# Expert weights: a place's down matrix is loaded behind the next place's gate and up matrices

## The chip, the cores and the metric

The kernel runs on one core of one Trainium2 chip. The metric is device time in microseconds (us) of one launch, as the median over several runs. Profile times count from the start of the profiled span. Engines are named as the profile names them: PE (TensorE, matrix products), DVE (VectorE), ACT (ScalarE), POOL (GpSimd), SP (SyncE, which here issues nearly all weight loads); "SPq" in a row is SP's own instruction stream.

## What is computed

One step of a one-layer decoder for 512 prompt tokens and 32 sample tokens: a combined input projection, an mLSTM branch, a windowed attention branch, a merge, a layer norm, a mixture of experts, a second norm, a gated embedding, a third norm. The change lies in the mixture of experts alone:

```
def expert_block(args):
    xblk, e = args
    h = jax.nn.silu(xblk @ w_gate[e]) * (xblk @ w_up[e])
    return h @ w_down[e]
...
y = jnp.zeros((M + 1, D), jnp.float32).at[row_tok].add(yb.reshape(P, D).astype(jnp.float32) * row_w[:, None])
```

There are 32 experts. Each token goes to two of them, so 544 tokens make 1088 rows. Of one expert the gate and the up matrix are 1024 x 512 in float32 and the down matrix is 512 x 1024: three times 2 MB.

## The kernel before

**Places, slots, items.** The experts that have tokens are put in an order that the chip works out from the routing; position p in it is a "place". Here there are 27 places, 0 to 26. Each place has one or more "items" of up to 32 rows; 50 items in all. A place's weights lie in one of `NB = 4` slots of SBUF, and place p uses slot p mod 4 as far as place 23; the last three places, 24 to 26, use slots 1, 2 and 3. In the profile, slots 0 and 1 are both called `w`; slot 2 is `w2a` (gate and up, first half of the contraction), `w2b` (second half) and `w2d` (down); slot 3 is `gu3a`, `gu3b` and `r_p`. The loads of places 0 to 3 are issued ahead of the loop; this document speaks of places 4 to 26.

**What TensorE does.** `items_of` walks through the items of a place. For one item, `gate_up` multiplies the first half (32 products, line L299), then the second half (32 more). Then comes the down product (`down`, 16 products, L310) of the item *before* this one: if the item is not the first of its place, that is an item of the same place and needs the same place's down matrix; if it is the first, it is the last item of the place before. So TensorE frees a slot in the order: first gate/up half (semaphore `gh`), second half (`gu`), and, one item later, the down matrix (`dn`). TensorE waits for weights by slot: `gu`*s* and `gv`*s* for the two gate/up halves, `wd`*s* and `we`*s* for the two halves of the down matrix.

**What SP does.** One load is 1 MB; gate and up of one half are two loads (`load_gu`, L135), the down matrix two loads (`load_dn`, L141). `load_place(s, p, before)` reads the number of the expert and the count of items up to the last place of this slot (`value`, L185), waits until TensorE has done so many first halves, issues 2 MB, waits for so many second halves, issues 2 MB, waits for the down product, issues 2 MB. It is called for places 4, 5, 6, ... in turn: a loop `Fori` over full turns of four slots, then straight code for the last, possibly partial turn (`gap` says how many slots it leaves out; here 1). SP works in order, so each wait also holds up every load behind it. Once the last place is loaded, SP issues the `late` loads (L229), and after the experts' last stores the tail begins.

Of the kernel before, what the change touches and what calls it, by code (L numbers as in the profile page):

```python
# [42 lines left out]
NB = 4  # L43
# [88 lines left out]
def load_gu(eng, W, s, w, e, half):  # L132

    ks = slice(KD // 2 * half, KD // 2 * (half + 1))
    return [eng.dma_start(out=W[s][half][:, i], in_=w[i][bass.ds(e, 1)].rearrange("a (p k) f -> (a p) k f", p=P)[:, ks])  # L135
            for i in range(2)]


def load_dn(eng, W, s, w, e, half):
    ks = slice(2 * half, 2 * half + 2)  # L140
    return eng.dma_start(out=W[s][2][:, ks], in_=w[2][bass.ds(e, 1)].rearrange("a (p k) d -> (a p) k d", p=P)[:, ks])  # L141
# [10 lines left out]
def expert_phase(tc, pool, psum, ident, meta, slots, x1, W, w, ybuf, spare, gcol, late, rows, spreads, xs, any_):  # L152
# [12 lines left out]
    sp, pe, act, dve, gp = nc.sync, nc.tensor, nc.scalar, nc.vector, nc.gpsimd  # L165
# [14 lines left out]
    with tc.tile_critical(no_gpsimd_drain=True):  # L180
        S = {n: nc.alloc_semaphore("x_" + n) for n in names}

        def value(e, i, lo, hi, n=1):
            src = meta[0:1, i:i + n] if isinstance(i, int) else meta[0:1, bass.ds(i, n)]
            _, out = nc.values_load_multi_w_load_instructions(  # L185
                src, engines=[e.engine], min_val=lo, max_val=hi,
                skip_runtime_bounds_check_because="the chip made it within bounds")
            return out if n > 1 else out[0]
# [6 lines left out]
            d.then_inc(S[f"gv{NB - 1}"], 16)  # L195
        npos, turns, gap = value(sp, 80, NB, 32), value(sp, 81, 0, 32 // NB - 1), value(sp, 84, 0, NB - 1)

        def load_place(s, p, before):
            e = value(sp, p, 0, 31)
            cnt = value(sp, before, 1, 66)  # L200
            for half, n in enumerate(("gu", "gv")):
                sp.wait_ge(S["gh" if half == 0 else "gu"], cnt)
                for d in load_gu(sp, W, s, w, e, half):
                    d.then_inc(S[f"{n}{s}"], 16)
            sp.wait_ge(S["dn"], sp.snap(cnt + 1))
            for half, n in enumerate(("wd", "we")):
                load_dn(sp, W, s, w, e, half).then_inc(S[f"{n}{s}"], 16)

        with sp.If(turns > 1):
            with sp.Fori(1, turns) as a:  # L210
                for s in range(NB):
                    p = sp.snap(a * NB + s)
                    load_place(s, p, sp.snap(p + (41 - NB)))
        with sp.If(turns > 0):
            for s in range(NB):
                def load_last():
                    p = sp.snap(npos - (NB - s))
                    load_place(s, p, sp.snap(p + gap + (41 - NB)))

                if s < NB - 1:  # L220
                    with sp.If(gap < s + 1):
                        load_last()
                else:
                    load_last()

        for s, loads in late:
            sp.wait_ge(S["dn"], sp.snap(value(sp, sp.snap(npos + (41 - NB + s)), 1, 66) + 1))
# [133 lines left out]
        npp, full, gap = value(pe, 80, NB, 32), value(pe, 81, 0, 32 // NB - 1), value(pe, 84, 0, NB - 1)  # L361
# [8 lines left out]
        for s in range(NB):  # L370
            p = pe.snap(npp - (NB - s))
# [145 lines left out]
def tile_decoder_step(ctx: ExitStack, tc: tile.TileContext, *aps):  # L517
# [1546 lines left out]
    with ExitStack() as scope:  # L2064

        SP_ = pool("spare", stack=scope)
        spare = SP_.tile([P, D], F32, name="xg"), SP_.tile([P, 2, KD, P], F32, name="xg4")
        gather = gp.indirect_dma_start(out=spare[0], out_offset=None, in_=x1d[:], in_offset=bass.IndirectOffsetOnAxis(ap=tok0[:, 0:1], axis=0))
        with tc.issue_after(gather.ins):
            gp.tensor_copy(out=edge[:, 0:1], in_=r_p[:, 0, 0:1])  # L2070
        for _ in prefetch(3, (2,)):
            pass
        expert_phase(tc, pool("xwork", side="right", stack=scope), pool("expp", space=PSUM, stack=scope), ident, meta,
                     (tok, yrow, ywt, shift1, gain1), x1d[:], w_tiles, w_e, ybuf[:], spare, gcol8, late, gb, spreads, x1s,
                     keep[:, 0:256])
# [225 lines left out]
```

## Time and profile before

| | us |
|---|---|
| median of 3 runs | 1129.75 |
| lowest and highest | 1129.23, 1131.23 |
| the profiled execution's own time | 1130.72 |
| its span in the profile | 1128.8 |

The time of the profiled execution is 1.9 us more than its span and 1.0 us more than the median. The expert phase takes the span from about 654 to 1040 us. Ahead of it lie the projections and branches, bound by PE; behind it lies a tail of about 80 us.

Rows of a timeline read: start, duration, engine, line, operation, what is written and read, count, and in brackets the idle time of that engine just before with what ended it. Rows of windows give busy time and count of PE, PEld, DVE, ACT and POOL, then the granted PE clock, the DMA engines' share and GB/s.

### The profile page before, as it was taken

To read this page: it belongs to the slowest core of one execution; us is meant where nothing else is said; L and a number is where in the kernel's file an instruction comes from. 1 tells how busy PE (TensorE), PEld (TensorE's weight loads), DVE (VectorE), ACT (ScalarE), POOL (GpSimd) and SP (SyncE) were. 2 spreads that over 40 slices of the span, in tenths; PEclk is the share of its full clock that TensorE was granted. 3 is DMA by queue.
4 is the path that set the end of the run, shared out by engine and by line. 5 is a ranking of instruction groups with operands and counts; after the bars stand their busy time and mean duration, and the time that the engine had idled before them with its cause. 6 is when DMAs were issued, how large, how long until landed. Compare 5 with 4: busy or idle time off the path is not lost.

```text
span 1128.8 us, 26851 instructions
## 1 busy us (share of the span) xinstructions
PE 1024.6 (91%) x10341; PEld 825.0 (73%) x10342; DVE 494.2 (44%) x1255; ACT 346.8 (31%) x703; POOL 253.3 (22%) x387
## 2 busy tenths in 40 slices
PE   8999999999999999999999867685999778868887
PEld 8988999999877779999989435352666545545765
DVE  5545543546545555565565612110222112113787
ACT  5411223223576565423213211110222112103431
POOL 5000000401346462313401202210222202122021
PEclk9999999999999999999999989896999989889899
DMA  7222222223314323753396979999999999998711
GB/s 251 76 76 64 87 75 75 80 75 112 101 38 150 112 95 132 241 158 77 101 391 258 416 301 417 425 419 427 419 424 421 422 424 421 425 416 361 287 47 62
DMA packets 92305, 264.19 MB, mean 234 GB/s; under 512 B 11486, under 2 KB 58740, under 8 KB 71460
## 3 DMA queue, kind: packets, MB, share of 16 engines
q1 hardware_dynamic: 77332, 231.82, 53.3%
q0 software_dynamic: 10384, 27.67, 6.8%
q10 hardware_dynamic: 4512, 3.64, 1.1%
q8 instruction: 53, 0.87, 0.3%
q14 instruction: 24, 0.20, 0.0%
HBM read 248.96 MB, written 20.13 MB: 238 GB/s over the span
## 4 chain that ended last, share of the span: by engine, by line
PE 70%; DMA 14%; SPq 8%; DVE 4%; issue 4%; ACT 1%; DVEq 0%; POOL 0%; ACTq 0%; POOLq 0%
PE pj L674 14%; PE pj L676 13%; PE pj L675 13%; PE psG L299 9%; SPq L135 5%; DMA w2b<-in_w_eu_dram 5%; DMA gu3b<-in_w_eu_dram 5%; PE psY L310 4%; PE tp L1269 2%; SPq L141 2%; PE sp L1315 1%; PE nm L1303 1%; PE sp L732 1%; DMA w<-ybuf 1%; DMA wg_in<-in_w_in_dram 1%
## 5 line engine op out<-in xcount | busy, mean ns | idle before, releaser
L674 PE MATMUL pj<-xH,wH 128*128 128x256 f32 (+1 forms) x672 | 197.6, 294 | 0.1
L676 PE MATMUL pj<-xH,wL 128*128 128x256 f32 (+1 forms) x672 | 197.4, 294 | 0.0
L675 PE MATMUL pj<-xL,wH 128*128 128x256 f32 (+1 forms) x672 | 195.6, 291 | 0.0
L561 ACT CAST wH<-raw 128x1024 fp32r<-128x1024 f32 x76 | 79.7, 1048 | 232.3 <-PE pj L675 148.2
L674 PEld LDWEIGHTS pj<-xH,wH 128*128 128x128 f32 x672 | 126.5, 188 | 5.5 <-issue 3.8
L676 PEld LDWEIGHTS pj<-xH,wL 128*128 128x128 f32 x672 | 126.4, 188 | 5.5 <-issue 5.1
L675 PEld LDWEIGHTS pj<-xL,wH 128*128 128x128 f32 x672 | 127.1, 189 | 2.0 <-issue 1.5
L562 DVE TENSOR_TENSOR wL<-raw,wH 128x1024 fp32r<-128x1024 f32 x76 | 95.2, 1252 | 69.4 <-ACT wH L561 69.2
L448 DVE COPY xT<-xg 128x256 f32 x49 | 15.3, 313 | 246.1 <-PE psG L299 246.1
L422 ACT ACTIVATE sg<-psG 128x128 f32<-128x128 f32 x50 | 13.9, 277 | 270.9 <-PE psG L299 270.9
L299 PE MATMUL psG<-w,xT 128*32 128x256 f32 x1152 | 72.2, 406 | 25.0 <-issue 18.1
L299 PEld LDWEIGHTS psG<-w,xT 128*32 128x32 f32 x1152 | 43.2, 116 | 52.7 <-issue 34.5
L1291 POOL TENSOR_SCALAR lg<-lg,sm 128x256 f32<-128x256 f32 (+1 forms) x64 | 55.8, 884 | 32.6 <-DVE sm L1288 28.7
L264 POOL DMA_INDIRECT ybuf<-ysb,idy x50 | 49.9, 998 | 45.3 <-POOL idy L261 41.2
L299 PE MATMUL psG<-gu3a,xT 128*32 128x256 f32 x576 | 37.4, 402 | 14.7 <-DMA gu3a<-in_w_eu_dram 9.3
L299 PE MATMUL psG<-w2a,xT 128*32 128x256 f32 x448 | 32.1, 434 | 17.8 <-DMA w2a<-in_w_eu_dram 13.8
L674 PE MATMUL pj<-wH,xH 128*128 128x256 f32 x160 | 47.3, 296 | 0.0
L404 ACT ACTIVATE xg<-psX,gcol 128x128 f32 (+1 forms) x100 | 36.3, 469 | 31.4 <-PE psX L292 31.4
L676 PE MATMUL pj<-wH,xL 128*128 128x256 f32 x160 | 44.8, 280 | 0.0
L675 PE MATMUL pj<-wL,xH 128*128 128x256 f32 x160 | 44.8, 280 | 0.0
L299 PE MATMUL psG<-gu3b,xT 128*32 128x256 f32 x576 | 37.8, 405 | 6.8 <-DMA gu3b<-in_w_eu_dram 6.8
L299 PEld LDWEIGHTS psG<-gu3a,xT 128*32 128x32 f32 x576 | 20.7, 113 | 29.0 <-issue 22.2
(619 smaller groups left out, 2245.0 us busy)
## 6 DMA issues: line engine op xcount, KB each, us to landing
w<-in_w_eg_dram SPq DMA_DIRECT2D x26, 1024.0 KB, 24.0
w<-in_w_eu_dram SPq DMA_DIRECT2D x26, 1024.0 KB, 27.6
w<-in_w_ed_dram SPq DMA_DIRECT2D x26, 1024.0 KB, 28.5
raw<-in_w_in_dram SPq DMA_DIRECT2D x22, 1024.0 KB
w2d<-in_w_ed_dram SPq DMA_DIRECT2D x14, 1024.0 KB, 29.2
r_p<-in_w_ed_dram SPq DMA_DIRECT2D x14, 1024.0 KB, 27.3
w2a<-in_w_eg_dram SPq DMA_DIRECT2D x7, 1024.0 KB, 28.7
w2a<-in_w_eu_dram SPq DMA_DIRECT2D x7, 1024.0 KB, 28.4
```

The costliest lines, as they stand in the source:

```text
L135: return [eng.dma_start(out=W[s][half][:, i], in_=w[i][bass.ds(e, 1)].rearrange("a (p k) f -> (a p) k f", p=P)[:, ks]) for i in range(2)]
L141: return eng.dma_start(out=W[s][2][:, ks], in_=w[2][bass.ds(e, 1)].rearrange("a (p k) d -> (a p) k d", p=P)[:, ks])
L264: gp.indirect_dma_start(out=ybuf.rearrange("t (q d) -> (t q) d", q=4), out_offset=bass.IndirectOffsetOnAxis(ap=idy[:, r:r + 1], axis=0), i ...
L299: m = pe.matmul(psG[32 * q:32 * q + 32], xT[:, k], W[s][half][:, :, kh, P * q:P * q + P], start=k == 0, stop=k == KD - 1)
L310: m = pe.matmul(psY[32 * q:32 * q + 32], hT[:, 32 * k:32 * k + 32], W[s][2][:, k, 256 * q:256 * q + 256], start=k == 0, stop=k == 3)
L404: m = act.activation(out=out, in_=psX[:, k], func=AF.Identity, bias=gcol[:, 1, k:k + 1], scale=gcol[:, 0, k:k + 1])
L561: act.copy(out=H, in_=src)
L562: return eng.tensor_tensor(out=L, in0=src, in1=H.bitcast(F32), op=ALU.subtract)
L674: pe.matmul(out, lh(k), rh(k), start=start and i == 0, stop=False)
L675: pe.matmul(out, lh(k), rl(k), start=False, stop=False)
L676: pe.matmul(out, ll(k), rh(k), start=False, stop=stop and i == len(ks) - 1)
L1291: gp.tensor_scalar(out=lg[:, par, j, 0:nk], in0=lg[:, par, j, 0:nk], scalar1=sm[:, 2, par, j:j + 1], scalar2=None, op0=ALU.mult)
```

## The change

`load_place` is split into `load_up` (gate and up, both halves) and `load_down`. SP now issues, for each place p, first its gate and up matrices, and then the down matrix of place p-1, which lies in the slot before. The very first place of the loop has no down load behind it, and the last place's down load is issued by itself at the end. Waits, semaphores and loads are the same in number and kind; TensorE's, VectorE's, ScalarE's and GpSimd's programs are unchanged. SP reads two more values for each place.

```diff
-        def load_place(s, p, before):
+        def load_up(s, p, before):
             e = value(sp, p, 0, 31)
             cnt = value(sp, before, 1, 66)
             for half, n in enumerate(("gu", "gv")):
                 sp.wait_ge(S["gh" if half == 0 else "gu"], cnt)
                 for d in load_gu(sp, W, s, w, e, half):
                     d.then_inc(S[f"{n}{s}"], 16)
-            sp.wait_ge(S["dn"], sp.snap(cnt + 1))
+
+        def load_down(s, p, before):
+            e = value(sp, p, 0, 31)
+            sp.wait_ge(S["dn"], sp.snap(value(sp, before, 1, 66) + 1))
             for half, n in enumerate(("wd", "we")):
                 load_dn(sp, W, s, w, e, half).then_inc(S[f"{n}{s}"], 16)
...
                 for s in range(NB):
                     p = sp.snap(a * NB + s)
-                    load_place(s, p, sp.snap(p + (41 - NB)))
+                    load_full(load_up, s, p)
+                    if s:
+                        load_full(load_down, s - 1, sp.snap(p - 1))
+                    else:
+                        with sp.If(a > 1):
+                            load_full(load_down, NB - 1, sp.snap(p - 1))
...
+                with sp.If(gap < s + 1) if s < NB - 1 else nullcontext():
+                    load_last(load_up, s)
+                    if s:
+                        with sp.If(gap < s):
+                            load_last(load_down, s - 1)
+                    with sp.If((gap - s) * (gap - s) < 1):
+                        first_of_turn()
+            load_last(load_down, NB - 1)
```

On SP, in the loop, from the down load of slot 2 on (`w2d`) to the gate and up loads of slot 3 (`gu3a`, `gu3b`); place 22 is one that uses this slot 2, and place 23 follows it in slot 3. Before:

```order
L141 DMA w2d<-in_w_ed_dram 128x2048 [waits x_dn]
L141 DMA w2d<-in_w_ed_dram 128x2048
L185 ISA
L185 TENSOR_LOAD meta
L185 ISA
L185 TENSOR_LOAD meta
L135 ISA [waits x_gh]
L135 DMA gu3a<-in_w_eg_dram 128x2048
L135 DMA gu3a<-in_w_eu_dram 128x2048
L135 ISA [waits x_gu]
L135 DMA gu3b<-in_w_eg_dram 128x2048
L135 DMA gu3b<-in_w_eu_dram 128x2048
```

The same place in SP's program with the change:

```order
L135 ISA [waits x_gh]
L135 DMA gu3a<-in_w_eg_dram 128x2048
L135 DMA gu3a<-in_w_eu_dram 128x2048
L135 ISA [waits x_gu]
L135 DMA gu3b<-in_w_eg_dram 128x2048
L135 DMA gu3b<-in_w_eu_dram 128x2048
L185 TENSOR_LOAD meta x2
L208 REGISTER_ALU
L141 ISA [waits x_dn]
L141 DMA w2d<-in_w_ed_dram 128x2048
L141 ISA
L141 DMA w2d<-in_w_ed_dram 128x2048
```

The two down loads have moved behind four gate and up loads, and behind the two waits ahead of those (`x_gh`, `x_gu`).

On SP, the start of the loop: the end of slot 0's gate and up loads (`w_6264`), and what stands between them and the loads of slot 1 (`w_6265`). Before:

```order
L135 DMA w_6264<-in_w_eu_dram 128x2048
L205 REGISTER_ALU
L141 DMA w_6264<-in_w_ed_dram 128x2048 [waits x_dn]
L141 DMA w_6264<-in_w_ed_dram 128x2048
L185 ISA
L185 TENSOR_LOAD meta
L185 ISA
L185 TENSOR_LOAD meta
L135 ISA [waits x_gh]
L135 DMA w_6265<-in_w_eg_dram 128x2048
```

With the change, the block from the first branch to the second is jumped over in the loop's first turn:

```order
L135 DMA w_6264<-in_w_eu_dram 128x2048
L227 COMPARE_AND_BRANCH
L185 ISA
L185 TENSOR_LOAD meta
L185 ISA
L185 TENSOR_LOAD meta
L208 REGISTER_ALU
L141 ISA [waits x_dn]
L141 DMA r_p<-in_w_ed_dram 128x2048
L141 ISA
L141 DMA r_p<-in_w_ed_dram 128x2048
L227 UNCONDITIONAL_BRANCH
```

What follows at once there is the reading of values and the wait `x_gh` of slot 1: in the first turn SP no longer waits for a down product between the loads of place 4 and of place 5.

More of the change, by code (lines that the diff above doesn't have):

```diff
@@ L204, in load_place, with load_full, load_last @@
                     d.then_inc(S[f"{n}{s}"], 16)
-            sp.wait_ge(S["dn"], sp.snap(cnt + 1))
+        def load_down(s, p, before):
+            e = value(sp, p, 0, 31)
+            sp.wait_ge(S["dn"], sp.snap(value(sp, before, 1, 66) + 1))
             for half, n in enumerate(("wd", "we")):
                 load_dn(sp, W, s, w, e, half).then_inc(S[f"{n}{s}"], 16)
+        def load_full(load, s, p):
+            load(s, p, sp.snap(p + (41 - NB)))
+        def load_last(load, s):
+            p = sp.snap(npos - (NB - s))
+            load(s, p, sp.snap(p + gap + (41 - NB)))
         with sp.If(turns > 1):
@@ L212, in expert_phase, with first_of_turn @@
                     p = sp.snap(a * NB + s)
-                    load_place(s, p, sp.snap(p + (41 - NB)))
+                    load_full(load_up, s, p)
[4 more added lines that the diff above has]
+                            load_full(load_down, NB - 1, sp.snap(p - 1))
         with sp.If(turns > 0):
             for s in range(NB):
[L216 to L224, printed above, removed]
+                def first_of_turn():
+                    with sp.If(turns > 1):
+                        load_full(load_down, NB - 1, sp.snap((turns * NB + 31) & 31))
+                with sp.If(gap < s + 1) if s < NB - 1 else nullcontext():
[6 more added lines that the diff above has]
+            load_last(load_down, NB - 1)
         for s, loads in late:
```

## The prediction

> **What bounds the kernel now.** I began with the slices of the page, to see which resource is full where.
>
> ```profile
> PE   8999999999999999999999867685999778868887
> DMA  7222222223314323753396979999999999998711
> GB/s 251 76 76 64 87 75 75 80 75 112 101 38 150 112 95 132 241 158 77 101 391 258 416 301 417 425 419 427 419 424 421 422 424 421 425 416 361 287 47 62
> ```
>
> A slice is 28.2 us. From slice 24 on (about 677 us) the DMA engines move 416 to 427 GB/s until about 1020 us: full, whatever the order of the loads. So bytes set the rate, and the change adds none. What an order can change are three things: idle time at the start, the moment at which a given matrix lands, and idle time that comes when SP is held up. Next I read the start in windows of 2 us, with SP's and PE's rows.
>
> ```profile
> 670.00:672.00 2.00, 2.00 (x36) 1.18 (x32) 0.07 (x1) 0.28 (x1) 0.00 (x0) 0.87 0.87 365
> 672.00:674.00 2.00, 1.30 (x27) 0.54 (x16) 0.92 (x4) 0.00 (x0) 0.00 (x0) 1.00 0.17 66
> 674.00:676.00 2.00, 1.79 (x36) 1.35 (x40) 0.38 (x1) 0.00 (x0) 0.00 (x0) 1.00 0.86 201
> 676.00:678.00 2.00, 2.00 (x44) 1.48 (x40) 0.00 (x0) 0.07 (x1) 0.00 (x0) 1.00 0.98 406
> ```
>
> ```profile
> 661.76 0.43 SPq L135 DMA_DIRECT2D w<-in_w_eu_dram  x1
> 673.36 1.08 SPq L141 DMA_DIRECT2D w<-in_w_ed_dram  x2
> 675.44 0.33 SPq L135 DMA_DIRECT2D w<-in_w_eg_dram  x1
> ```
>
> ```profile
> 665.41 6.16 PE L299 MATMUL psG<-w,xT 128*32 128x256 f32 x64 [4.27 <-issue]
> 671.39 1.91 PE L310 MATMUL psY<-w,hT 128*32 128x256 f32 x32
> ```
>
> The engines run dry: against 422 GB/s the four windows lose (57 + 356 + 221 + 16) x 2 us = 1300 KB, or 3.1 us; I use 3.0. SP had issued place 4's gate and up by 662.2, then stood in the wait for place 0's down product, which ended at 673.30 (671.39 + 1.91). Place 1's gate/up product had freed its first half long before: 6.16 us from 665.41, the first half done at about 669. From issue at 673.36 to full flow after 676 pass about 2 us.
>
> Then the places. Items can be read off PE's rows: a second item of one place uses the same tiles. Place 11 has eight (`gu3a` from 782 to 830), place 22 has five (`w2a` from 961 to 994). Around place 22:
>
> ```profile
> 955.81 1.94 PE L310 MATMUL psY<-w,hT 128*32 128x256 f32 x32
> 960.80 3.52 PE L299 MATMUL psG<-w2a,xT 128*32 128x256 f32 x32 [3.05 <-DMA w2a<-in_w_eu_dram]
> 966.90 3.12 PE L299 MATMUL psG<-w2b,xT 128*32 128x256 f32 x32 [2.58 <-DMA w2b<-in_w_eu_dram]
> 969.77 2.47 PE L310 MATMUL psY<-w,hT 128*32 128x256 f32 x32
> 974.07 1.94 PE L299 MATMUL psG<-w2b,xT 128*32 128x256 f32 x32
> 975.80 1.94 PE L310 MATMUL psY<-w2d,hT 128*32 128x256 f32 x32
> ```
>
> These are the last waits of PE for a weight load. From 969.77 on PE works or waits for its own program, up to the last down product, the last store of rows and the tail:
>
> ```profile
> 1037.81 1.93 PE L310 MATMUL psY<-r_p,hT 128*32 128x256 f32 x32 [1.42 <-DVE ysb L460]
> 1041.61 1.47 POOL L264 DMA_INDIRECT ybuf<-ysb,idy  x1 [0.86 <-POOL idy L261]
> 1048.04 0.81 SPq L2099 DMA_DIRECT2D w<-ybuf  x2
> ```
>
> So the time follows from when place 22's first own down product is done (975.80 + 1.94 = 977.74): all behind it is a chain of PE, then the store, then the tail.
>
> **The change, term by term.** *Counts.* No load, wait or PE instruction is added; SP reads two more values for each place. In a full stretch its issues last 2 us and more since they wait for room, so this is hidden; if the queue were empty it would cost some 0.6 us (SP's rows around 675: 674.44 to 675.44 for two reads and their register work).
>
> *The gap at 672 (-3.0 us on every later landing).* SP now goes from place 4's loads straight to place 5's first half, free at about 669. That is 2 us before the queue runs dry, which is what a load needs to flow, so I take the whole gap as filled. Bounds: 0 if the gap only moves, -3.1.
>
> *Where each matrix lands.* Up to the end of the loop gate and up come 2 MB earlier and the down matrix 4 MB later. What 4 MB are worth here is read from place 22's down matrix and place 23's gate and up, which now go ahead of it. The issues, then the landing times of slot 2's down loads and of the second-half loads of slot 3:
>
> ```profile
> 940.03 4.47 SPq L141 DMA_DIRECT2D w2d<-in_w_ed_dram  x2
> 953.62 2.40 SPq L135 DMA_DIRECT2D gu3b<-in_w_eu_dram  x1
> ```
>
> ```profile
> L141 SPq DMA_DIRECT2D w2d<-in_w_ed_dram x2: 1986/2188/2390, 940.0 to 942.1; - x2
> DMA to landing us min/median/max: 29.3/29.4/29.6
> ```
>
> ```profile
> L135 SPq DMA_DIRECT2D gu3b<-in_w_eu_dram x1: 2398/2398/2398, 953.6 to 953.6; - x1
> DMA to landing us min/median/max: 28.0/28.1/28.2
> ```
>
> The down matrix landed at 942.1 + 29.6 = 971.7, place 23's last up load at 953.6 + 28.2 = 981.8. Taking the landing order as the order of issue, the down matrix now lands where that load did: 10.1 us later. The Trainium skill (DMA: Bandwidth & Descriptors, Queues, rings and completion order) says that each DMA engine consumes its ring in order, while completion is not ordered over the engines; by that the sum stays as it is, and the waits above, ended in the order of issue, agree.
>
> A place with one item loses nothing by that, since its down product comes after the next place's gate/up product anyway. A place with several items needs its own down matrix right after its second gate/up product. These are places 6, 8, 11, 14, 16, 19, 22 and 24. Most of it is paid back where PE later waits for gate and up, which now come earlier (3.05 and 2.58 us ahead of place 22). Place 22 is not followed by such a wait.
>
> *Place 11 (takes back about 2.4 of the 3.0).* Its eight items hold slot 3, and SP stands behind them:
>
> ```profile
> 787.17 3.30 PE L299 MATMUL psG<-gu3b,xT 128*32 128x256 f32 x32 [1.73 <-DMA gu3b<-in_w_eu_dram]
> 796.70 1.91 PE L310 MATMUL psY<-r_p,hT 128*32 128x256 f32 x32
> 809.89 4.18 SPq L141 DMA_DIRECT2D w2d<-in_w_ed_dram  x2
> 830.24 0.33 SPq L135 DMA_DIRECT2D gu3a<-in_w_eg_dram  x1
> ```
>
> ```profile
> 774.48 0.38 SPq L135 DMA_DIRECT2D w<-in_w_eu_dram  x1
> w<-in_w_eu_dram SPq DMA_DIRECT2D x1, 1024.0 KB, 29.0
> ```
>
> ```profile
> L141 SPq DMA_DIRECT2D w2d<-in_w_ed_dram x2: 2017/2043/2069, 809.9 to 812.0; - x2
> DMA to landing us min/median/max: 29.1/29.2/29.4
> ```
>
> Place 11's down matrix will land with what was place 12's last up load, 774.48 + 29.0 = 803.5, less 3.0: 800.5. PE has then idled for some us and its clock is low: the product at 787.17 took 3.30 where a warm one takes 1.94, so I price half a down product at 1.75 us instead of 0.87. Done at 802.2 against 798.6 before: place 11 ends 3.6 us later, and SP issues place 15's gate load at 833.8 instead of 830.24. Ahead of that load stood 2 MB of place 14's down matrix (landed at 812.0 + 29.4 = 841.4); these now stand behind it. So the queue is dry at 841.4 - 5.0 (half of the 10.1 above) - 3.0 = 833.4, while the next data flow at 833.8 + 2.0 = 835.8: a gap of 2.4 us. Bounds: 0 if data flow as soon as issued, or 4.9, since that 833.4 is the last engine's landing and most may be dry 2.5 us earlier (half of a 2 MB load). I take 2.4, nearest to the gap that the rows at 672 show for the same hold-up. Left of the gain: 0.6 us.
>
> *Place 22 (+5.2 us).* Its down matrix lands at 981.8 - 0.6 = 981.2. PE has its second gate/up product done at about 974 (place 19 delays it in the same way) and stands still for some 5 us to the first half, so the second half is at the low clock: 981.2 + 1.75 = 982.95. Before it was 977.74. Bounds: 981.8 - 3.0 + 0.87 = 979.7 (+1.9; no gap at place 11, warm clock), and 981.8 + 1.9 + 1.75 = 985.45 (+7.7; a gap of 4.9).
>
> *Behind it (0).* The same dry queue can come at place 22's release (about 997), but what it delays has room: the last down matrix is used at 1037.81 + 5.2.
>
> ```profile
> L141 SPq DMA_DIRECT2D r_p<-in_w_ed_dram x2: 928/1337/1746, 1005.7 to 1007.1; - x2
> DMA to landing us min/median/max: 26.1/26.6/27.2
> ```
>
> It landed at 1007.1 + 27.2 = 1034.3, 3.5 us ahead of its use, and the delay gives it 5.2 us more. The tail starts when the last store has landed, which moves with PE.
>
> **Sum.** Against the profiled execution (1130.72): +5.2, so 1135.9. It stands 0.97 above the median of the runs, so in terms of the median 1129.75 + 5.2 = 1134.95, say **1135.0 us**.
>
> **Rivals.**
> - *The stall is absorbed (no change).* Of the same mechanism only the low end: the 3.0 us are kept whole and the clock stays warm, +1.9, 1131.65. For it: the place-11 gap hangs on 2.4 us between two estimates. Against: after idle of that length PE's rows are slow (3.52 at 960.80). It decides at a gap of about 0.4 us, if the clock is warm.
> - *Faster: the gap at 672 is all that counts.* The loads move up by 3.0 us and so does PE, if place 22's down matrix does not become the last wait: 1126.75. It needs that matrix to land by 977.74 - 0.87 - 3.0 = 973.9, that is within 2.2 us of before, though 4 MB go ahead of it; only if loads in flight overtake one another. The Trainium skill (Perfetto Trace Analysis, Optimization Strategy) says to look for the gaps on the engine that should be saturated and to make what blocks it start sooner; by that alone the change is a gain of this size, and the trace agrees as to the gap.
> - *Slower still.* The dry stretch at place 11 is larger and place 19 (five items) adds its own, so that PE comes late to place 22: 8 to 10 us, about 1138.8. For it: SP holds 2 MB fewer in the queue at each release.
> - *The change does nothing.* Excluded as to order: the two listings differ. As to time it falls under the first rival.
>
> **Chances.** A difference under 0.2% (2.3 us) can't be told from none. Forecast (+2.3 to +8) 0.70; slower still 0.06; no change 0.16; faster 0.08. So slower 0.76, same 0.16, faster 0.08. The range reaches from just under the lower bound (1131.65) to just above the upper (1137.45): 1130.5 to 1138.5.
>
> **What would show it.** No dip of GB/s at 672 to 676; the first load of place 5 issued at about 669. PE waits that end on `r_p<-in_w_ed_dram` near 800 and on `w2d<-in_w_ed_dram` near 981, in front of L310, where there were none; shorter waits for `w2a` and `w2b`. A dip of the DMA share near 834. The last L310 product at about 1043. The forecast is wrong if PE shows no wait for a down load, or if the queue stays full at 834 and the last product comes before 1040.

## The result, and the profile after

| | before | changed |
|---|---|---|
| median, us | 1129.49 (6 runs) | 1137.54 (6 runs) |
| lowest and highest | 1129.03, 1131.23 | 1135.51, 1139.48 |
| profiled execution, its span | 1130.72, 1128.8 | 1139.48, 1137.6 |

The ratio is 1.0067, with a 95% interval of 1.0056 to 1.0078: the change makes the kernel slower by about 8 us. The profiled execution of the changed kernel is 1.9 us above its median, so sizes read from its trace are on the high side. The ratios and medians in this document leave out one execution of 2504.75 us, of the last kernel that keeps the gap. Line numbers of the changed kernel are 18 higher: L299 is now L317, L310 is L328, L2099 is L2117. A down product is 32 matrix products in these rows, 16 for each half of its matrix; the 16 given above for the whole of it is the count of calls in the program.

First the page, with the rate of the DMA engines in slices (28.4 us each now):

```profile
GB/s 249 76 75 68 82 74 75 80 75 119 92 38 149 111 102 139 222 158 89 122 414 253 390 377 420 422 422 425 421 306 421 423 423 423 419 326 410 291 48 61
```

Before, the slices from 24 to 35, counted from 0, were all between 416 and 427. Now two are holes: slice 29 (825 to 853 us) at 306 GB/s and slice 35 (995 to 1024) at 326. Next the start in windows of 2 us, of the changed kernel:

```profile
670.00:672.00 2.00, 2.00 (x44) 1.28 (x40) 0.45 (x2) 0.28 (x1) 0.00 (x0) 1.00 1.01 426
672.00:674.00 2.00, 1.07 (x24) 0.46 (x18) 0.93 (x3) 0.00 (x0) 0.00 (x0) 1.00 1.01 414
```

The dip of before (66 GB/s in the second window) is gone. The same view of the first new hole:

```profile
826.00:828.00 2.00, 1.77 (x36) 0.78 (x24) 0.58 (x3) 1.25 (x2) 1.22 (x2) 1.00 0.97 397
828.00:830.00 2.00, 1.88 (x36) 1.43 (x40) 0.81 (x2) 0.31 (x1) 1.18 (x2) 1.00 0.57 227
830.00:832.00 2.00, 2.00 (x44) 1.42 (x38) 0.00 (x0) 0.12 (x1) 0.98 (x1) 1.00 0.34 137
832.00:834.00 2.00, 1.74 (x34) 0.98 (x29) 0.85 (x3) 0.16 (x1) 0.00 (x0) 1.00 0.17 66
834.00:836.00 2.00, 2.00 (x44) 1.47 (x40) 0.54 (x2) 0.00 (x0) 0.18 (x1) 1.00 0.00 0
836.00:838.00 2.00, 2.00 (x44) 1.47 (x40) 0.14 (x1) 0.28 (x1) 0.98 (x1) 1.00 0.63 119
838.00:840.00 2.00, 1.17 (x24) 0.51 (x15) 0.81 (x4) 0.00 (x0) 0.00 (x0) 1.00 0.92 365
```

The flow does not stop at once: it falls over some 8 us, and stands at 0 only for the last two. SP's own timeline shows why:

```profile
669.67 0.34 SPq L135 DMA_DIRECT2D w<-in_w_eg_dram  x1
...
803.42 3.52 SPq L141 DMA_DIRECT2D w<-in_w_ed_dram  x2
835.90 0.33 SPq L135 DMA_DIRECT2D gu3a<-in_w_eg_dram  x1
...
1056.76 0.81 SPq L2117 DMA_DIRECT2D w<-ybuf  x2
```

Place 5's first load goes out at 669.67, no longer at 675.44. But between 806.94 (803.42 + 3.52) and 835.90 SP stands for 29.0 us in the wait for place 11 to free slot 3. Before, place 14's down matrix was issued until 814.07 and the stand lasted 16.2 us. In the kernel before a load landed 28 to 30 us after its issue, so a stand of 29 us drains the queue, and there one of 16 us did not.

PE's timeline at the two places that the prediction speaks of, and at the last down product:

```profile
801.69 1.93 PE L328 MATMUL psY<-r_p,hT 128*32 128x256 f32 x16 [0.39 <-DMA r_p<-in_w_ed_dram]
803.57 2.93 PE L317 MATMUL psG<-gu3a,xT 128*32 128x256 f32 x32
...
982.16 1.07 PE L328 MATMUL psY<-w2d,hT 128*32 128x256 f32 x16 [3.00 <-DMA w2d<-in_w_ed_dram]
984.92 1.93 PE L328 MATMUL psY<-w2d,hT 128*32 128x256 f32 x16 [1.70 <-DMA w2d<-in_w_ed_dram]
986.79 3.47 PE L317 MATMUL psG<-w2a,xT 128*32 128x256 f32 x32
...
1047.62 1.93 PE L328 MATMUL psY<-r_p,hT 128*32 128x256 f32 x32 [1.42 <-DVE ysb L478]
```

Place 22's down product, which before ran without a wait and was done at 977.74, now waits for each half of its matrix and is done at 986.85, 9.1 us later. The last down product ends 9.8 us later (1049.55 against 1039.74), and the tail begins 8.7 us later (1056.76 against 1048.04). Part of the difference is the last store of rows: it landed 3.33 us after its issue at 1051.91, before 5.33 us after 1041.61.

PE's waits for expert loads from 650 to 1060 us, in us in total, their count and the longest. Before:

```profile
PE psG L299 <- DMA w2a<-in_w_eu_dram: 13.8, 4, 5.2
PE psG L299 <- DMA gu3a<-in_w_eu_dram: 9.3, 2, 4.9
PE psG L299 <- DMA w2b<-in_w_eu_dram: 9.2, 4, 4.3
PE psG L299 <- DMA gu3b<-in_w_eu_dram: 6.8, 3, 3.7
PE psG L299 <- DMA w<-in_w_eu_dram: 6.3, 2, 5.0
```

With the change:

```profile
PE psY L328 <- DMA r_p<-in_w_ed_dram: 17.2, 5, 8.3
PE psY L328 <- DMA w2d<-in_w_ed_dram: 16.1, 7, 8.3
PE psY L328 <- DMA w<-in_w_ed_dram: 10.3, 5, 7.1
PE psG L317 <- DMA gu3b<-in_w_eu_dram: 4.5, 2, 2.8
PE psG L317 <- DMA gu3a<-in_w_eu_dram: 3.9, 2, 2.4
PE psG L317 <- DMA w2b<-in_w_eu_dram: 0.4, 1, 0.4
```

Before, all 45.4 us were waits for gate and up. Now those are 8.8 us, and 43.6 us are waits for a down matrix. The waits have changed their kind, and their sum has grown by 7.0 us to 52.4.

### The profile page after: what moved, and what is told of

It is laid out like the page before. It is cut to its first block, busy times and chain, and to the rows that moved or that the text cites. A ratio compares the mean times of both kernels' runs of the same rounds, so it can differ in the third digit from the quotient of the medians.

```text
span 1137.6 us, 26974 instructions
## 1 busy us (share of the span) xinstructions
PE 1024.2 (90%) x10341; PEld 823.1 (72%) x10342; DVE 494.4 (43%) x1255; ACT 346.8 (30%) x703; POOL 253.7 (22%) x387
## 4 chain that ended last, share of the span: by engine, by line
PE 69%; DMA 11%; SPq 11%; issue 4%; DVE 4%; ACT 1%; DVEq 0%; POOL 0%; POOLq 0%; ACTq 0%
PE pj L692 13%; PE pj L694 13%; PE pj L693 13%; PE psG L317 9%; SPq L135 6%; DMA r_p<-in_w_ed_dram 5%; PE psY L328 4%; SPq L141 4%; DMA w2d<-in_w_ed_dram 2%; PE tp L1287 2%; PE sp L1333 1%; PE nm L1321 1%; PE sp L750 1%; DMA w<-ybuf 1%; DMA xg<-x1d,tok 1%
## 5 line engine op out<-in xcount | busy, mean ns | idle before, releaser
L317 PE MATMUL psG<-w,xT 128*32 128x256 f32 x1152 | 69.1, 393 | 20.4 <-issue 19.8
L317 PEld LDWEIGHTS psG<-w,xT 128*32 128x32 f32 x1152 | 42.3, 113 | 45.9 <-issue 28.9
L471 DVE STREAM_TRANSPOSE hT<-h 128x128 f32<-128x128 f32 x50 | 20.5, 410 | 101.3 <-PE psY L328 101.2
L328 PE MATMUL psY<-r_p,hT 128*32 128x256 f32 x576 | 38.9, 408 | 20.0 <-DMA r_p<-in_w_ed_dram 17.2
L328 PE MATMUL psY<-w,hT 128*32 128x256 f32 x576 | 36.7, 390 | 10.3 <-DMA w<-in_w_ed_dram 10.3
L328 PEld LDWEIGHTS psY<-r_p,hT 128*32 128x32 f32 x576 | 21.4, 115 | 33.8 <-DMA r_p<-in_w_ed_dram 20.4
L317 PE MATMUL psG<-gu3a,xT 128*32 128x256 f32 x576 | 37.6, 404 | 9.0 <-issue 4.9
L328 PE MATMUL psY<-w2d,hT 128*32 128x256 f32 x448 | 30.4, 407 | 16.1 <-DMA w2d<-in_w_ed_dram 16.1
```

What stands on the lines that cost most here:

```text
L317: m = pe.matmul(psG[32 * q:32 * q + 32], xT[:, k], W[s][half][:, :, kh, P * q:P * q + P], start=k == 0, stop=k == KD - 1)
L328: m = pe.matmul(psY[32 * q:32 * q + 32], hT[:, 32 * k:32 * k + 32], W[s][2][:, k, 256 * q:256 * q + 256], start=k == 0, stop=k == 3)
```

## The experiments

All ratios are to the kernel before, measured beside it (its medians were 1129.23 and, twice, 1130.02), with 95% intervals. Differences in us are 1130 times the ratio's distance from 1; the medians give up to 1.2 us less or more. The question is how the 8 us divide between three terms: the gap at 672, the late landing of a down matrix that its own place needs, and the dry stretch behind place 11.

### The control: the old order in the new code

SP's program has the two functions and the extra reads, in the order of before:

```diff
                     load_full(load_up, s, p)
-                    if s:
-                        load_full(load_down, s - 1, sp.snap(p - 1))
-                    else:
-                        with sp.If(a > 1):
-                            load_full(load_down, NB - 1, sp.snap(p - 1))
+                    load_full(load_down, s, p)
...
-            load_last(load_down, NB - 1)
+                    load_last(load_down, s)
```

> The order of before, written with the changed kernel's two functions, so that SP reads the two further values for each place. Theory A (order alone costs): within 1 us of before. Theory C (SP's longer program costs a part of the 8 us): slower than before by 1 us or more.

Measured: 1130.19 us, ratio 0.9999 (0.9989 to 1.0009). The longer program on SP costs nothing that can be seen (about 1 us at most); the 8 us come from the order.

### The gap at 672 alone

The order of before, except that in the loop's first turn place 5's gate and up go ahead of place 4's down:

```diff
+                    if s == 0:
+                        with sp.If(a > 1):
+                            load_full(load_down, s, p)
+                    else:
+                        if s == 1:
+                            with sp.If(a < 2):
+                                load_full(load_down, 0, sp.snap(p - 1))
+                        load_full(load_down, s, p)
...
+                    load_last(load_down, s)
```

> The old order everywhere but at the start: place 5's gate and up ahead of place 4's down, then both downs; from place 6 on each place's down behind its own gate and up. Theory A (the new order costs because a place with several items gets its own down matrix 4 MB later, and because SP is held up behind a place with many items; the filled gap at 672 us by itself is a gain): no gap at 672, no gap at 828 to 840, all landings 3 us earlier, 2.5 to 3.1 us faster than before, about 1126.7. Theory B (the filled gap does harm or is lost anyway further down, since TensorE and not the loads sets the pace): within 1 us of before. Theory C (SP's longer program, with more reads of values, is what costs): slower than before by 1 us or more.

Measured: 1127.55 us, 0.998 (0.9971 to 0.9988), 2.2 us faster, a little less than the 2.5 expected at least. The windows of this run:

```profile
672.00:674.00 2.00, 2.00 (x43) 1.19 (x36) 0.49 (x2) 0.28 (x1) 0.00 (x0) 0.97 0.92 311
674.00:676.00 2.00, 1.09 (x24) 0.49 (x19) 0.89 (x2) 0.00 (x0) 0.00 (x0) 1.00 0.93 340
```

About 0.9 us of the gap stays here ((422 - 311 + 422 - 340) x 2 / 422), and 2.2 us are gained of the 3.0. So the gap is worth close to what it loses, as long as nothing else is moved. The Trainium skill (Perfetto Trace Analysis, Optimization Strategy) says to find the gaps on the engine one optimizes for and to make what blocks it start sooner; this run agrees with it. The changed kernel closes the same gap and is slower, so for the whole change the measurement decides.

### Two terms taken away singly and together

Two edits of the changed kernel, each at one place of the loop. The first sends place 14's down ahead of place 15's gate and up, so that SP has issued these 2 MB before it stands behind place 11. The second sends place 22's down ahead of place 23's gate and up, so that it does not land late; its condition has `a - 5` (place 23) where the one shown has `a - 3` (place 15).

```diff
+                    if s == 3:
+                        with sp.If((a - 3) * (a - 3) < 1):
+                            load_full(load_down, s - 1, sp.snap(p - 1))
                     load_full(load_up, s, p)
-                    if s:
+                    if s == 3:
+                        with sp.If((a - 3) * (a - 3) > 0):
+                            load_full(load_down, s - 1, sp.snap(p - 1))
+                    elif s:
                         load_full(load_down, s - 1, sp.snap(p - 1))
```

The first alone:

> The changed order, but at place 15 alone place 14's down load stands ahead of place 15's gate and up, so that SP does not hold 2 MB back while it waits for place 11's eight items. Theory A (two costs, hold-up and late landing): the gap at 828 to 840 is gone or under 1 us, place 22's down matrix lands about 3 us earlier than in the changed kernel, 4 to 6 us slower than before (1134 to 1136). Theory B (the hold-up is the whole loss): no slower than before, about 1127 to 1130. Theory C (the late landing is the whole loss, the gap costs nothing): like the changed kernel, about 8 us slower than before.

The second alone:

> The changed order, but at place 23 alone place 22's down load stands ahead of place 23's gate and up, so that the five items of place 22 get their own down matrix as early as in the old order. Theory A (two costs): the gap at 828 to 840 stays, PE's wait for place 22's down matrix falls from 4.7 us to under 1, and 2 to 4 us slower than before are left (1131.5 to 1133.5). Theory B (the hold-up is the whole loss): like the changed kernel, 8 us slower. Theory C (the late landing of place 22's down matrix is the whole loss): no slower than before, 1127 to 1130.

Both (the condition is the product of the two):

> The changed order, but at places 15 and 23 alone the down load of the place before stands first: no hold-up behind place 11, and place 22's own down matrix as early as in the old order. Theory A (these two places make up the loss): no gap at 828 to 840, none at 995 to 1005, 0.5 to 2 us faster than before (1127 to 1128.7); less than 3 us because places 11 and 19 still wait for their own down matrices. Rival (the loss is spread over all places with several items): 2 us or more slower than before.

| | dry stretch at place 11 | place 22's down late | us | ratio |
|---|---|---|---|---|
| both edits | no | no | 1127.98 | 0.9981 (0.9972 to 0.999) |
| first alone | no | yes | 1132.7 | 1.0031 (1.0019 to 1.0044) |
| second alone | yes | no | 1131.21 | 1.0021 (1.001 to 1.0033) |
| neither: the changed kernel | yes | yes | 1137.54 | 1.0067 (1.0056 to 1.0078) |

Late landing costs 0.0050 where there is no dry stretch (5.6 us) and 0.0046 where there is one (5.2 us). The dry stretch costs 0.0040 (4.5 us) without late landing and 0.0036 (4.1 us) with it. Each difference is uncertain by about 0.0015; within that the terms add up. A second measurement of the changed kernel (below) gave 1.0078; with it the late landing costs 0.0057 where there is a dry stretch, and the dry stretch 0.0047 where there is late landing. With both taken away what is left is a gain of 2.1 us, as large as that of the gap alone, so nothing that these intervals would show (1.5 us) is left over for places 6 to 19, whose down matrices land late too. The first edit's 3.5 us are just below the 4 to 6 that theory A named; its rivals B (no slower than before) and C (8 us) are excluded. The windows, first the changed kernel:

```profile
822.00:842.00 20.00, 18.02 (x321) 11.68 (x323) 4.63 (x13) 5.02 (x12) 6.00 (x10) 1.00 0.66 255
984.00:1008.00 24.00, 21.72 (x336) 12.89 (x340) 5.13 (x14) 5.02 (x12) 5.01 (x9) 0.88 0.76 301
```

With the first edit alone:

```profile
822.00:842.00 20.00, 18.02 (x332) 11.96 (x328) 4.50 (x14) 3.12 (x8) 4.74 (x9) 1.00 0.96 392
```

With both edits:

```profile
822.00:842.00 20.00, 18.06 (x328) 11.86 (x324) 4.14 (x12) 4.26 (x11) 5.79 (x9) 1.00 0.95 386
984.00:1008.00 24.00, 16.07 (x288) 10.18 (x280) 4.22 (x12) 3.31 (x8) 6.25 (x11) 1.00 0.98 404
```

The "no" of the table is not quite one: against 422 GB/s the windows with the first edit and with both still lose 1.4 and 1.7 us of full flow, as SP stands for 23 to 24 us there. With the second edit alone the first hole is there, and place 22's down product still has no wait in front of it; one row of each view:

```profile
822.00:842.00 20.00, 18.02 (x332) 11.98 (x324) 4.55 (x14) 3.07 (x7) 4.70 (x8) 1.00 0.76 300
```

```profile
976.63 1.94 PE L334 MATMUL psY<-w2d,hT 128*32 128x256 f32 x32
```

With both edits that product starts at 973.32, so here the dry stretch makes it 3.3 us later.

### The second hole

Each edit that leaves place 22's down late also leaves a hole at 984 to 1008. To see whether the hole itself costs anything, the first edit is joined with a third: place 24's down goes ahead of place 25's gate and up, so that SP has issued 2 MB more before it stands behind place 22, while place 22's down still lands late.

```diff
+                    if s == 2:
+                        with sp.If(gap < s):
+                            load_last(load_down, s - 1)
                     load_last(load_up, s)
-                    if s:
+                    if s and s != 2:
```

> The changed order, but at places 15 and 25 alone the down load of the place before stands first: SP holds nothing back behind place 11 nor behind place 22, so both dry stretches go, while every place with several items still gets its own down matrix 4 MB later. Theory A (the second dry stretch, at 995 to 1005, delays nothing that is on the path): like the run with place 15 alone, 3 to 4.5 us slower than before. Rival (the second dry stretch costs too, through the last loads): 2 us or more faster than the run with place 15 alone.

Measured: 1133.28 us, 1.0029 (1.002 to 1.0039). The window of the first edit alone, then of this kernel:

```profile
984.00:1008.00 24.00, 21.22 (x375) 13.73 (x368) 5.53 (x16) 5.30 (x13) 6.65 (x12) 1.00 0.73 290
```

```profile
984.00:1008.00 24.00, 21.24 (x372) 13.61 (x364) 5.62 (x16) 5.30 (x13) 6.81 (x12) 1.00 0.98 402
```

The hole is filled (290 to 402 GB/s) and the time is the same, 1.0031 against 1.0029. So the second hole costs nothing that can be seen (the ratios are uncertain by 0.0015, 1.7 us), and the 5 us are those of the late landing: in this kernel too the product waits.

```profile
976.01 1.93 PE L337 MATMUL psY<-w2d,hT 128*32 128x256 f32 x16 [4.01 <-DMA w2d<-in_w_ed_dram]
978.43 1.94 PE L337 MATMUL psY<-w2d,hT 128*32 128x256 f32 x16 [0.48 <-DMA w2d<-in_w_ed_dram]
```

It is done at 980.37, against 975.26 (973.32 + 1.94) with the first and second edits: 5.1 us.

### Is the 3.0 us gain still in the changed kernel?

The changed order, but with the gap at 672 left open (place 4's down ahead of place 5's gate and up):

```diff
-                    if s:
-                        load_full(load_down, s - 1, sp.snap(p - 1))
-                    else:
+                    if s == 0:
+                        with sp.If(a < 2):
+                            load_full(load_down, 0, p)
                         with sp.If(a > 1):
                             load_full(load_down, NB - 1, sp.snap(p - 1))
+                    elif s == 1:
+                        with sp.If(a > 1):
+                            load_full(load_down, s - 1, sp.snap(p - 1))
+                    else:
+                        load_full(load_down, s - 1, sp.snap(p - 1))
```

> The changed order from place 5 on, but place 4's down load stands ahead of place 5's gate and up as before, so that the gap at 672 us comes back. Theory A (what the filled gap gains is kept to the end, since place 11 is then later by as much and the dry stretch behind it as long): 2 to 3 us slower than the changed kernel, about 1140. Rival (the dry stretch at 828 to 840 swallows the gain, so that nothing of it is left): within 1 us of the changed kernel's 1137.5, with a dry stretch some 3 us shorter.

Measured: 1139.55 us, 1.0079 (1.0065 to 1.0094), against 1.0067 for the changed kernel in its own comparison. Since the intervals overlap, the pair was measured again side by side, the changed kernel as it is:

> The changed kernel itself, for a comparison on one chip with the next run: 7 to 8.5 us slower than before.

and the kernel with the gap:

> The changed order with the gap at 672 us kept, beside the changed kernel on the same chip. Theory A (the gain of the filled gap is kept): 2 to 3 us slower than the changed kernel. Rival (the dry stretch behind place 11 swallows it): within 1 us of it.

Measured: 1137.61 us, 1.0078 (1.0064 to 1.0091), and 1140.23 us, 1.0091 (1.0076 to 1.0107). By the ratios both pairs differ by 0.0012 to 0.0013, 1.4 us; by the medians the second pair differs by 2.6 us. In both pairs the intervals overlap: half of the gain or more seems to be kept in the changed kernel, but this stays unsettled. One way in which it could be lost is ruled out by the windows of the second pair, the changed kernel first: the hole behind place 11 is equally large with the gap and without it.

```profile
822.00:842.00 20.00, 18.01 (x328) 11.88 (x324) 4.14 (x12) 3.54 (x9) 5.43 (x9) 1.00 0.73 286
```

```profile
822.00:842.00 20.00, 18.02 (x319) 11.78 (x321) 4.82 (x14) 5.02 (x12) 6.00 (x10) 1.00 0.72 285
```

### An order by need

If the theory holds, a down matrix should go behind the next place's gate and up only where its own place has one item. SP reads the count of items of place p-1 and decides; the straight code for the last places keeps the changed order:

```diff
+                    def guarded(several):
+                        first, end = value(sp, sp.snap(p + 39), 0, 66, 2)
+                        n = sp.snap(sp.snap(end) - sp.snap(first))
+                        with sp.If(n > 1) if several else sp.If(n < 2):
+                            load_full(load_down, (s - 1) % NB, sp.snap(p - 1))
...
+                    guarded(True)
                     load_full(load_up, s, p)
+                    guarded(False)
```

> The order in which TensorE needs the matrices: behind a place with several items its own down matrix comes first and then the next place's gate and up; behind a place with one item the changed order. SP reads the number of items for it. Theory A: no wait of PE for a down matrix over 2 us, no gap at 672 nor at 828, 2.5 to 3.2 us faster than before, about 1126.7. Theory B (SP's longer program costs, or any down load behind gate and up costs): slower than before by 1 us or more.

Measured: 1127.18 us, 0.9978 (0.9968 to 0.9989). It is 2.5 us faster than the kernel before and 10 faster than the changed one, but no faster than the old order with the gap filled (0.9980) or the changed order with both edits (0.9981). PE's waits for a down matrix, and the last down product:

```profile
PE psY L342 <- DMA w<-in_w_ed_dram: 4.1, 5, 1.4
PE psY L342 <- DMA w2d<-in_w_ed_dram: 3.8, 4, 1.4
PE psY L342 <- DMA r_p<-in_w_ed_dram: 2.1, 2, 1.5
```

```profile
1031.05 2.04 PE L342 MATMUL psY<-r_p,hT 128*32 128x256 f32 x32 [1.42 <-DVE ysb L492]
```

PE's waits for a down matrix fall from 43.6 us in the changed kernel to 10.0, none longer than 1.5; those for gate and up are 28.8, so that 38.8 stand against 45.4 before. The last down product ends at 1033.09, 6.65 us before that of the kernel before. The tail starts only 3.15 us sooner (1044.89 against 1048.04). The chain of work that ended last shows what holds it now (start, duration, what), and SP's timeline the tail:

```profile
1019.76 24.52 DMA w<-in_w_pg_dram
```

```profile
1044.89 0.81 SPq L2131 DMA_DIRECT2D w<-ybuf  x2
```

This last of the `late` loads lands 24.5 us after its issue, at 1044.3, right before the tail. In the kernel before it landed at 1046.6 (issued at 1022.39, 24.2 us), only 0.4 us ahead of the last store of rows; here it lands 2.3 us earlier, about what the filled gap gains, and PE's further lead is hidden behind it. To see what the end of the loads costs, the same kernel with that load cut short:

```diff
-    (*pg_half(0), "al")
+    (pg_half(0)[0][:, 0:1], pg_half(0)[1][:, 0:1], "al")
```

> The order of need again, and of the last load that is issued behind the experts' weights (half of w_pg, 2 MB, for the tail) only an eighth is loaded; so the gate of the last stage is computed from other data. In the run with the order of need TensorE's last down product ended 6.6 us before that of the kernel before, but the tail began only 3.2 us earlier, with the landing of this load. Theory A (there the end of the loads has taken over from TensorE): the tail begins 2 to 4 us earlier than in the order of need, 4 to 6 us faster than before. Rival (something else holds the start of the tail): within 1 us of the order of need, about 2 us faster than before.

Measured: 1126.3 us, 0.9969 (0.9957 to 0.9981), about 1 us better, which the intervals do not tell from none; in the profile the tail begins 0.9 us earlier, not 2 to 4. So the load is not the whole limit. In this run the next holder is VectorE, which waits for the norm's gain (`r_s`, one of the `late` loads too) until 1038.66 and is done at 1043.29, ahead of a tail that starts at 1044.02. With the load in full VectorE was done at the same time, 1043.31, 1.0 us before that load landed:

```profile
1038.66 4.63 DVE L542 TENSOR_TENSOR w<-w,r_s 128x1024 f32<-128x1024 f32 x4 [4.01 <-DMA r_s<-in_ln_g_dram]
```

So PE's 6.65 us can be had only in part: behind PE, the `late` loads are the next to hold the tail.

## Why the prediction was right, and which of its terms was too small

It forecast a loss, by this mechanism, of 5.2 us; measured are 8.0 us by the medians and 7.6 by the ratio, within the range and 1 us from its upper end. In the same terms the forecast was -3.0 (gap), +5.8 (place 22's late landing) and +2.4 (dry stretch); the table gives -2.1, +5.2 to +5.6 and +4.1 to +4.5.

- **Counts (0).** Right: the control is at 0.9999.
- **The gap at 672 (-3.0).** Right in place and time (669.67 against the 669 predicted). Worth 2.2 us alone and 2.1 us with both other terms removed, so it was somewhat too large; beside the other terms 1.4 to 2.6 us of it are seen.
- **The landing order.** Right. Place 11's second half-product started at 801.69, and at 800.33 in the second profiled execution (the changed kernel measured again, 1136.10 us), which bounds its landing (800.5 predicted). With the dry stretch taken away, place 22's down landed at 978.4 in the kernel with the third edit, where 981.8 - 3.0 = 978.8 was the prediction. No wait ended as if loads in flight had overtaken one another, which the "faster" rival needed.
- **Place 22 (+5.2, of which 2.8 without a dry stretch).** The part without a dry stretch is 981.8 - 3.0 + 1.75 = 980.55 against 977.74, 2.8 us net; the first edit alone and with the third measured 3.5 and 3.3 net (0.0031 and 0.0029 of 1130). Nearly right. The cold clock was priced close to what the profiled execution shows (1.93 for a half product, 1.75 predicted), but the sum stops at the down product, and the gate/up half behind it is slow too: 3.47 us at 986.79 and 2.93 at 803.57, against 1.9 when warm. That price is not paid each time: in the second profiled execution place 22's second half took 1.07 us. One step was off and did not enter the sum: PE was to stand for 5 us from about 974; it had its second gate/up product done at 979.16 (977.22 + 1.94) and stood for 3.00 and 1.70 us. The matrix still landed last, so the landing alone set the time.
- **Place 11's dry stretch (+2.4). This is the term that was mis-sized: it cost 4.1 to 4.5 us.** The step that failed is that the queue was taken to be full up to 833.4, the landing of its last load. In the windows the flow falls from 826 on: up to 836 they lose 6.1 us of full flow, as much as a queue that is dry from 829.9; in the second execution, where SP issues again at 833.77, the windows from 826 to 834 (342, 211, 90 and 0 GB/s) lose 5.0 us, as if dry from 829.0. That is 3.5 to 4.4 us earlier than was taken. SP's hold-up was right in one execution and short in the other: priced at 833.8, place 15's load went out at 833.77 in the second profiled execution and at 835.90 in the first, where place 11's down product was done at 803.62, not 802.2, and the slow gate/up half behind it added 1 us. In all, the stretch from 822 to 842 lost (422 - 255) x 20 / 422 = 7.9 us of full flow in the first execution and (422 - 286) x 20 / 422 = 6.4 in the second. The upper bound of 4.9, for engines that are "dry 2.5 us earlier", held the price; choosing its middle did not. Of that lost flow, the kernels without the hold-up still lose 1.4 to 1.7 us. With the second edit alone, against both, the difference is (386 - 300) x 20 / 422 = 4.1 us, as much as the stretch costs; for the changed kernel against the first edit it is 5.0 and 6.5, and why these are above 4.1 to 4.5 is not shown.
- **Behind it (0).** Right: the second hole was forecast at place 22's release, came there, and costs nothing that can be seen.

Missed among the rivals was the mixture: "slower still" had the right sign for the dry stretch, but gave place 19 a part; the four kernels of the table account for the loss with places 11 and 22 alone, and from 840 to 980 the changed kernel moves 423 GB/s, as much as before, so place 19 brings no dry stretch.

## What to carry to other kernels

When loads go through one queue in order, the order of landing must follow the order of need of each item: a matrix with an early user that is moved behind one with a late user lands later by all that now goes ahead (here 4 MB, 10 us, of which 5 reached its product), and closing a gap of 3 us elsewhere does not pay for it. What stands behind a long wait on the issuing engine counts as much: here 2 MB moved from ahead of the wait to behind it, with a release that came 4 to 6 us later, turned a hold-up of 16 us into one of 28 to 29, longer than what the queue holds. Where the work per place varies, the program can read it and choose the order; here that avoided the loss, but gained no more than filling the gap alone.

## What the runs showed of the hardware that was not expected

- A queue that is fed no more does not end at once. From 397 GB/s in the window at 826, the rate fell to 227, 137, 66 and 0 over 8 us, and the engines' busy share with it, from 0.97 to 0. The last landing thus tells when the queue is empty, not until when it is full. Stands of SP of 23 to 24 us already lost 1.4 and 1.7 us of full flow (first edit, both edits).
- After the last window at 0, the new load issued at 835.90 brought 119 GB/s in 836 to 838 and 365 in 838 to 840: about 4 us from issue to nearly full flow. Against 422 GB/s the windows from 836 on lose 1.8 us, so as a price the 2.0 of the prediction held.
- The lower clock outlasts the wait. Windows of the changed kernel around place 22, then the two whole stretches at the lower clock, behind place 11's wait and place 22's (PE's granted clock is the third number from the end):

```profile
982.00:983.30 1.30, 1.07 (x16) 0.42 (x16) 0.00 (x0) 0.00 (x0) 0.00 (x0) 0.93 1.06 441
984.90:986.90 2.00, 1.98 (x20) 0.73 (x24) 0.00 (x0) 0.00 (x0) 0.00 (x0) 0.50 1.00 422
```

```profile
795.39:805.63 10.24, 5.88 (x52) 2.32 (x56) 0.89 (x2) 0.00 (x0) 0.19 (x1) 0.50 1.01 416
983.13:989.95 6.82, 5.12 (x52) 2.36 (x52) 0.89 (x2) 0.00 (x0) 0.00 (x0) 0.50 1.01 424
```

The first half product, after 3.0 us of waiting, still ran at nearly full clock and took 1.07 us; the second, after 1.7 us more, ran at 0.50 and took 1.93; the gate/up half behind it took 3.47. The clock fell at 983.13, 4.0 us after PE had stopped, and came back at 989.95, 5.0 us after work had resumed at 984.92. The two stretches are 10.24 and 6.82 us long, three and two times 3.41 us. The Trainium skill (TensorE: Matmul & The Clock Gate, What's actually happening) has the clock at half after an idle window of about 3.4 us, and at full again only after as much sustained work; the lengths agree with steps of such a window, but the window that ended at 983.13 was not idle throughout, since it held the first half product.
